# Seven block products for the FFN up projection, down steps between them, modulation sums on the tensor engine

## The chip, the cores and the metric

The kernel runs on one core of one Trainium2 chip. The metric is device time in microseconds (us) of one execution, from several runs. TensorE (PE) multiplies matrices into PSUM; VectorE (DVE), ScalarE (ACT) and GpSimd (POOL) work on elements; the DMA queue of SyncE (SP) brings data from DRAM.

## What is computed

Two layers of a diffusion backbone in float32: 512 tokens x and 256 context tokens, width 1024. A layer is a half-step FFN, a mixer (convolution, gated linear attention, attention), and another half-step FFN. The context's last FFN is not needed, so of four FFNs three have 768 tokens and the last has 512. Cut to what the change touches:

```python
def pre(x, mod, j, g):
    return rms_norm(x, g) * (1 + mod[:, :, 3 * j + 1]) + mod[:, :, 3 * j]

def half_ffn(x, mod, j, g, w1, w2):
    gu = pre(x, mod, j, g) @ w1          # w1: 1024 x (2 x 2816)
    a, u = jnp.split(gu, 2, axis=-1)
    return x + 0.5 * mod[:, :, 3 * j + 2] * ((jax.nn.silu(a) * u) @ w2)

mod_x = (silu(c) @ w_ada[i] + b_ada[i]).reshape(B, 1, 9, 1024)   # and mod_c of c_ctx
```

## The kernel before, in words

Tokens lie along the columns, features along the 128 partitions; 1024 features are eight K tiles. Every float32 matrix product is made of three passes over exact pairs (hi, lo) of reduced float32 (fp32r): hi x hi, hi x lo, lo x hi (`mm3`, L386). A weight tile of 128 x 1024 is loaded by `load_split` (L132): a DMA, a cast on ACT (hi), a subtraction on DVE (lo); three such pairs are in flight.

An FFN (`ffn`, L402) runs over 22 hidden tiles of 128. For each, `up` makes two tiles, a and u: 8 K tiles x 3 passes x 2 column pieces of 386 and 384 columns (768 tokens and two columns that carry the shift). `evac` (L462) multiplies by 1 / rms on DVE and applies silu or the shift on ACT; a product on DVE gives the hidden tile, which is split into a pair (gh, gl). After every two hidden tiles, `down` adds those of the pair before to all eight output tiles (528 matmuls of 512 columns and 528 of 256 per FFN, 528 of 512 in the last) and `add_gated` (L395) adds them to the residual xt on DVE. `Scale` (L336) prepares x * gs as pairs tile by tile as x becomes final.

The modulation vectors (`ada`, L183) are products of a vector by a matrix: ACT scales each K tile of 128 x 512 by its element of silu(c), DVE adds it up, and at the end TensorE sums over partitions (L206). Vectors 2 to 8 of layer 0 are made during the first FFN, 0 to 4 of layer 1 during the second, 5 to 8 during the third. `ada_first` (L211) makes vectors 1 and 0 on TensorE at the start; the first up products begin before the shifts (vector 0) are there (`Head`, `up_head`).

The order on each engine is set by the framework's scheduler, by the order of writing; only stretches under `manual_schedule` keep their written order on TensorE.

```python
    def mm3(outs, w, m, segs, first, last):
        for o, (t0, n) in zip(outs, segs):
            nc.tensor.matmul(out=o, lhsT=w[0], rhs=m[0][:, t0:t0 + n], start=first, stop=False)
        for o, (t0, n) in zip(outs, segs):
            nc.tensor.matmul(out=o, lhsT=w[0], rhs=m[1][:, t0:t0 + n], start=False, stop=False)
```

## Time and profile before

| | us |
|---|---|
| median of 3 runs | 2859.18 |
| lowest and highest run | 2856.81, 2865.5 |
| span of the profiled execution | 2857.3 |
| TensorE busy, of the span | 2781.7 |
| VectorE busy | 1768.5 |
| ScalarE busy | 1200.8 |
| GpSimd busy | 136.4 |

The page gives no time of the profiled execution beside its span, first to last instruction; the median of the runs is 1.9 us above the span. "Busy" of an engine is the union of its instructions; the mean of one matmul includes its overlap with the next, so the rate of matmuls is read from their starts. PEclk is the granted clock of TensorE (1.00 is 2.4 GHz, 0.5 is 1.2 GHz).

### The profile page before, as it was taken

To read this page: it belongs to the slowest core of one execution; us is meant where nothing else is said; L and a number is where in the kernel's file an instruction comes from. 1 tells how busy PE (TensorE), PEld (TensorE's weight loads), DVE (VectorE), ACT (ScalarE), POOL (GpSimd) and SP (SyncE) were. 2 spreads that over 40 slices of the span, in tenths; PEclk is the share of its full clock that TensorE was granted. 3 is DMA by queue.
4 is the path that set the end of the run, shared out by engine and by line. 5 is a ranking of instruction groups with operands and counts; after the bars stand their busy time and mean duration, and the time that the engine had idled before them with its cause. 6 is when DMAs were issued, how large, how long until landed. Compare 5 with 4: busy or idle time off the path is not lost. (4 is left out here: it accounts for less than half of the span.)

```text
span 2857.3 us, 42932 instructions
## 1 busy us (share of the span) xinstructions
PE 2781.7 (97%) x17498; PEld 2541.2 (89%) x17498; DVE 1768.5 (62%) x2974; ACT 1200.8 (42%) x1908; POOL 136.4 (5%) x134
## 2 busy tenths in 40 slices
PE   8999999999899999999999999999999989999999
PEld 4999999988687899999999999999997768999998
DVE  4786874464897565566465746454546588555555
ACT  4665662233347454254252523232324447432322
POOL 1000000010300100000000100000001110100000
PEclk9999999999999999999999999999999999999999
DMA  7443441221211243233231313231312131222322
GB/s 255 144 144 129 141 130 60 67 93 58 65 43 27 86 139 101 82 118 107 78 118 56 116 66 111 74 119 60 98 57 84 47 88 28 91 89 95 98 97 89
DMA packets 98501, 267.67 MB, mean 94 GB/s; under 512 B 11520, under 2 KB 11904, under 8 KB 98304
## 3 DMA queue, kind: packets, MB, share of 16 engines
q1 hardware_dynamic: 98304, 264.93, 28.7%
q8 instruction: 137, 2.24, 0.3%
q14 instruction: 60, 0.49, 0.1%
HBM read 249.16 MB, written 7.34 MB: 90 GB/s over the span
## 5 line engine op out<-in xcount | busy, mean ns | idle before, releaser
L137 ACT CAST whi<-raw 128x1024 fp32r<-128x1024 f32 (+1 forms) x314 | 324.6, 1044 | 1110.8 <-PE up L391 524.2
L389 PE MATMUL up<-sh,whi 128*128 128x386 f32 (+1 forms) x2808 | 691.4, 327 | 2.2 <-ACT sh L362 1.2
L391 PE MATMUL up<-sl,whi 128*128 128x386 f32 (+1 forms) x2808 | 687.8, 325 | 4.7 <-DVE sl L363 4.7
L393 PE MATMUL up<-sh,wlo 128*128 128x386 f32 (+1 forms) x2808 | 686.0, 325 | 0.1
L465 DVE TENSOR_TENSOR upv<-up,rb 128x770 f32<-128x770 f32 (+2 forms) x177 | 157.2, 889 | 639.0 <-PE up L393 634.7
L389 PEld LDWEIGHTS up<-sh,whi 128*128 128x128 f32 x2808 | 493.1, 190 | 12.4 <-ACT whi L137 4.2
L391 PEld LDWEIGHTS up<-sl,whi 128*128 128x128 f32 x2808 | 495.9, 190 | 7.5 <-DVE sl L363 7.3
L393 PEld LDWEIGHTS up<-sh,wlo 128*128 128x128 f32 x2808 | 494.1, 190 | 2.1 <-DVE upv L465 1.7
L399 DVE SCALAR_TENSOR_TENSOR xt<-dn,mods,xt 128x512 f32<-128x512 f32 (+1 forms) x616 | 375.2, 632 | 123.0 <-PE dn L393 122.3
L389 PE MATMUL dn<-gh,whi 128*128 128x512 f32 (+1 forms) x1232 | 429.9, 349 | 3.3 <-DVE xt L399 3.2
L138 DVE TENSOR_TENSOR wlo<-raw,whi 128x1024 fp32r<-128x1024 f32 (+1 forms) x314 | 378.6, 1215 | 83.3 <-ACT whi L137 75.1
L391 PE MATMUL dn<-gl,whi 128*128 128x512 f32 (+1 forms) x1232 | 427.7, 347 | 0.0
L393 PE MATMUL dn<-gh,wlo 128*128 128x512 f32 (+1 forms) x1232 | 426.4, 347 | 0.0
L195 ACT ACTIVATE adat<-adaw,sc 128x512 f32<-128x512 f32 x392 | 258.9, 715 | 84.0 <-DVE adacc L197 76.7
L389 PEld LDWEIGHTS dn<-gh,whi 128*128 128x128 f32 x1232 | 232.8, 189 | 45.0 <-ACT whi L137 7.9
L393 PEld LDWEIGHTS dn<-gh,wlo 128*128 128x128 f32 x1232 | 232.9, 189 | 31.2
L391 PEld LDWEIGHTS dn<-gl,whi 128*128 128x128 f32 x1232 | 233.0, 189 | 29.5
L197 DVE TENSOR_TENSOR adacc<-adacc,adat 128x512 f32<-128x512 f32 x392 | 250.4, 684 | 7.9 <-ACT adat L195 6.3
L468 ACT ACTIVATE upv<-upv 128x512 f32<-128x512 f32 (+1 forms) x308 | 179.7, 625 | 33.8 <-DVE upv L465 33.6
L389 PE MATMUL pj<-nh,whi 128*128 128x512 f32 (+1 forms) x328 | 120.5, 371 | 8.5 <-DVE var L572 4.3
L263 POOL TENSOR_TENSOR acc<-acc,sq 128x512 f32<-128x512 f32 (+1 forms) x72 | 76.1, 1057 | 1075.1 <-ACT sq L260 1069.7
L391 PE MATMUL pj<-nl,whi 128*128 128x512 f32 (+1 forms) x328 | 120.9, 369 | 2.4 <-DVE nl L332 2.3
(216 smaller groups left out, 2798.7 us busy)
## 6 DMA issues: line engine op xcount, KB each, us to landing
raw<-in_w_dram SPq DMA_DIRECT2D x264, 512.0 KB, 3.5
adaw<-in_wada_dram SPq DMA_DIRECT2D x288, 256.0 KB, 3.3
raw<-in_wt_dram SPq DMA_DIRECT2D x26, 512.0 KB, 3.4
raw<-in_wo_dram SPq DMA_DIRECT2D x16, 512.0 KB, 3.6
raw<-in_wk_dram SPq DMA_DIRECT2D x8, 416.0 KB, 3.2
xt<-in_xT_dram SPq DMA_DIRECT2D x8, 384.0 KB, 7.9
park<-xt SPq DMA_DIRECT2D x8, 384.0 KB, 2.3
xt<-park SPq DMA_DIRECT2D x8, 384.0 KB, 5.2
```

The lines of the kernel that those rows point to most:

```text
L137: nc.scalar.copy(out=hi[:, :n], in_=r[:, :n])
L138: nc.vector.tensor_tensor(out=lo[:, :n], in0=r[:, :n], in1=hi[:, :n].bitcast(F32), op=ALU.subtract)
L195: nc.scalar.activation(out=t, in_=r, func=AF.Copy, scale=sc[:, k, v:v + 1])
L197: nc.vector.tensor_tensor(out=acc[v], in0=acc[v], in1=t, op=ALU.add)
L263: eng.tensor_tensor(out=self.acc[:, t0:t0 + n], in0=self.acc[:, t0:t0 + n], in1=s[:, :n], op=ALU.add)
L389: nc.tensor.matmul(out=o, lhsT=w[0], rhs=m[0][:, t0:t0 + n], start=first, stop=False)
L391: nc.tensor.matmul(out=o, lhsT=w[0], rhs=m[1][:, t0:t0 + n], start=False, stop=False)
L393: nc.tensor.matmul(out=o, lhsT=w[1], rhs=m[0][:, t0:t0 + n], start=False, stop=last)
L399: nc.vector.scalar_tensor_tensor(out=x, in0=o[:, :n], scalar=mods[l][:, v, mod * KT + d:mod * KT + d + 1], in1=x, op0=ALU.mult, op1=ALU.add)
L465: nc.vector.tensor_tensor(out=a[:, t0:t0 + n], in0=p[:, c0:c0 + n], in1=rb[:, t0:t0 + n], op=ALU.mult)
L468: nc.scalar.activation(out=a[:, c], in_=a[:, c], func=AF.Silu if t == f else AF.Identity, bias=a[:, NX + v:NX + v + 1])
```

## The change

The up projection is seen as a product of 2 x 2 blocks: weights in rows a and u and in lower and upper half of K (four K tiles each), activations in the two halves of K and two halves of the tokens. Seven block products and sums before and after replace the eight products (`Combos` makes the sums T1 to T4 of activations, `Feed.ups` those of weights on POOL, `Up.product` the sums of results). Each product is 4 K tiles x 3 passes of half the tokens: 386 columns (258 in the last FFN). The sums of results are made in place: a later product accumulates on a PSUM bank that ACT or DVE has written. The order is a list, `PLAN`, in which single down steps (one output tile) stand between products; all engines keep the written order in an FFN. The first two products of the first four hidden tiles come first. 1 / rms is now multiplied on halves, and two columns of shifts ride with each half; the first products need the shifts. Weights lie in rings of their own: units of 128 x 512, five for up and three for down, four raw tiles.

The modulation sums are made on TensorE: four K tiles at a time, each into its own strip of 32 partitions, then a small matmul adds the strips. Constants that only the mixer needs are loaded there. In the mixer, weight splits are in halves of 512; the output projection runs in two token halves.

The core of the diff, first the modulation:

```diff
-                for v in range(nv):
-                    t = acc[v] if k == 0 else slot("F", "adat", (P, 512))
-                    nc.scalar.activation(out=t, in_=r, func=AF.Copy, scale=sc[:, k, v:v + 1])
-                    if k:
-                        nc.vector.tensor_tensor(out=acc[v], in0=acc[v], in1=t, op=ALU.add)
...
+            for k, r in enumerate(nxt):
+                nc.tensor.matmul(out=ps[32 * k:32 * k + 32, :], lhsT=spad[:, 2 * (4 * b + k):][:, :32], rhs=r, start=b == 0,
+                                 stop=b == 1, skip_group_check=True, tile_position=(0, 32 * k))
...
+                for s in range(4):
+                    nc.tensor.matmul(out=ps[:, 2 * s:2 * s + 2], lhsT=a[:, s * P:(s + 1) * P], rhs=sev,
+                                     start=True, stop=True, skip_group_check=True)
```

The sums of activations (`combine`), of weights (`sums`, `one`) and of results (`Up.product`):

```diff
+            def sums():
+                t.append(slot("E", "t13", (P, 2, self.w)))
+                nc.vector.tensor_tensor(out=t[0][:, 0], in0=a[:, 0], in1=b[:, 0], op=ALU.subtract)
+                nc.gpsimd.tensor_tensor(out=b[:, 0], in0=a[:, 1], in1=t[0][:, 0], op=ALU.subtract)
+                nc.vector.tensor_tensor(out=t[0][:, 1], in0=a[:, 1], in1=a[:, 0], op=ALU.subtract)
+                nc.gpsimd.tensor_tensor(out=b[:, 1], in0=b[:, 1], in1=b[:, 0], op=ALU.subtract)
+                self.pair(1, "xt", t[0], tags["13"], ("T1", "T3"), p)
...
+                s1[f] = slot("q", "s1", (P, 512))
+                pool(s1[f], ru[:, lo], ru[:, hi], ALU.add)
+                pool(ru[:, lo], ra[:, lo], ru[:, lo])
...
+                if r == 0:
+                    u = unit(ra[:, lo])
+                    pool(ra[:, lo], s1[f], ra[:, lo])
+                elif r == 1:
+                    u = unit(ra[:, hi])
+                    pool(ra[:, hi], ra[:, hi], ra[:, lo])
...
+                o, name = ((a, "11"), (b, "21"), (d, "T1"), (a, "T2"), (a, "T3"), (c, "22"), (a, "T4"))[r]
+                prod(o, x[name], r in (0, 2))
+                if r == 0:
+                    nc.scalar.copy(out=b, in_=a)
+                elif r == 1:
+                    mul(v0, b, rf[0])
+                elif r == 2:
+                    nc.scalar.copy(out=z[:, 1], in_=d)
+                    if b is not None and self.own:
+                        silu(v0[:, :nh], v0[:, nh:nh + 1])
+                elif r == 3:
+                    add(c, a, z[:, 1])
+                elif r == 4:
+                    add(z[:, 1], a, z[:, 1])
+                    mul(z[:, 1], z[:, 1], rf[1])
+                elif r == 5:
+                    mul(y[:, 1], c, rf[1])
+                else:
+                    for t, n, v in n1:
+                        silu(y[:, 1, t:t + n], (y[:, 1] if v else v0)[:, nh:nh + 1])
+                    mul(z[:, 0], a, rf[0])
+                    gate(z[:, 0, :nh], z[:, 0, nh:nh + 1], v0[:, :nh])
+                    for t, n, v in n1:
+                        gate(z[:, 1, t:t + n], z[:, v, nh:nh + 1], y[:, 1, t:t + n])
```

The product itself, the order, and the weight units:

```diff
+        def prod(o, b, start, post=None):
+            (hi, lo), = feed.get(1)
+            for p in range(4):
+                ws = slice(p * P, (p + 1) * P)
+                for e, (w, m) in enumerate(((hi, b[p][0]), (hi, b[p][1]), (lo, b[p][0]))):
+                    nc.tensor.matmul(out=o, lhsT=w[:, ws], rhs=m, start=start and p == 0 and e == 0,
+                                     stop=p == 3 and e == 2, skip_group_check=True)
...
+        seq = [("h1", f) for f in range(HEADS)] + [("h2", f) for f in range(HEADS)]
...
+            for f in fs:
+                for r in prods:
+                    add(f, r)
+                    if r in (3, 5, 0 if 2 * c >= HEADS else 6) or r == 2 and f > 2:
+                        seq.append(downs.popleft())
+                late.append(("g", f))
...
+        w = wp.tile([P, 2, 512], F32R, tag=tag, name=tag, bufs=RING if tag == "w" else DRING)
+        split(w[:, 0, :n], w[:, 1, :n], src)
```

How the instructions stand now, at three places. **TensorE, inside an FFN.** `up` is a PSUM bank, sh and sl (x22) are activations, whi and wlo (w) a weight pair. Before, the end of one tile and the beginning of the next:

```order
L389 MATMUL up_5231<-sh7_164,whi_5227 128x386
L389 MATMUL up_5231<-sh7_164,whi_5227 128x384
L391 MATMUL up_5231<-sl7_172,whi_5227 128x386
L391 MATMUL up_5231<-sl7_172,whi_5227 128x384
L393 MATMUL up_5231<-sh7_164,wlo_5228 128x386
L393 MATMUL up_5231<-sh7_164,wlo_5228 128x384
L389 MATMUL up_5295<-sh0_157,whi_5291 128x386
L389 MATMUL up_5295<-sh0_157,whi_5291 128x384
```

In the change, the end of the fifth product of a hidden tile, the sixth, the small modulation matmuls and the beginning of a down step:

```order
L649 MATMUL up_521<-xth_610,w_1129 128x386
L649 MATMUL up_521<-xtl_611,w_1129 128x386
L649 MATMUL up_521<-xth_610,w_1129 128x386
L649 MATMUL up_697<-x22_472,w_1164 128x386 x3
L649 MATMUL up_697<-x22_488,w_1164 128x386 x3
L649 MATMUL up_697<-x22_543,w_1164 128x386 x3
L649 MATMUL up_697<-x22_577,w_1164 128x386 x3
L214 MATMUL adapt_1323<-glb_75,adasb_1212 128x2 x4
L461 MATMUL dn_1330<-gh_1043,wd_516 128x512
L463 MATMUL dn_1330<-gl_1044,wd_516 128x512
```

One piece of 386 columns stands where two pieces of 386 and 384 stood, four K tiles make a product, and a down step or modulation work stands between products.

**VectorE, inside an FFN**, before (first FFN; adacc and adat are modulation, wlo a weight's low part, upv an up tile, gl a hidden tile's low part):

```order
L138 TENSOR_TENSOR wlo_783<-raw_780,whi_782 128x1024
L465 TENSOR_TENSOR upv_709<-up_660,rb_173 128x770
L138 TENSOR_TENSOR wlo_842<-raw_839,whi_841 128x1024
L197 TENSOR_TENSOR adacc_903<-adacc_903,adat_911 128x512
L197 TENSOR_TENSOR adacc_904<-adacc_904,adat_914 128x512
L423 TENSOR_TENSOR upv_643<-upv_709,upv_643 128x770
L197 TENSOR_TENSOR adacc_903<-adacc_903,adat_919 128x512
L197 TENSOR_TENSOR adacc_904<-adacc_904,adat_922 128x512
L197 TENSOR_TENSOR adacc_903<-adacc_903,adat_927 128x512
L143 TENSOR_TENSOR gl_715<-upv_643,gh_714 128x770
```

In the change (upz and upy are results of products, rinv is 1 / rms, up and dn are PSUM banks):

```order
L153 TENSOR_TENSOR w_1559<-raw_1264,w_1559 128x512
L655 TENSOR_TENSOR upz_1384<-up_697,upz_1384 128x386
L656 TENSOR_TENSOR upz_1384<-upz_1384,rinv_192 128x386
L153 TENSOR_TENSOR w_1577<-s1_1456,w_1577 128x512
L656 TENSOR_TENSOR upy_1383<-up_521,rinv_192 128x386
L472 SCALAR_TENSOR_TENSOR xt2_198<-dn_1581,mods0_78,xt2_198 128x512
L472 SCALAR_TENSOR_TENSOR xt2_198<-dn_1589,mods0_78,xt2_198 128x256
L153 TENSOR_TENSOR w_1609<-raw_1264,w_1609 128x512
L656 TENSOR_TENSOR upz_1384<-up_697,rinv_192 128x386
L658 SCALAR_TENSOR_TENSOR upz_1384<-upz_1384,upy_1383 128x384
L658 SCALAR_TENSOR_TENSOR upz_1384<-upz_1384,upy_1383 128x128
L658 SCALAR_TENSOR_TENSOR upz_1384<-upz_1384,upy_1383 128x256
```

The modulation sums are gone; between the low parts of weights stand sums of results, and the residual adds of one down step stand between those of two products.

**GpSimd**, before, from the end of the sums for the second FFN's norm to those for the third's (attm belongs to the second layer's mixer):

```order
L263 TENSOR_TENSOR acc_9041<-acc_9041,sq_9477 128x256
L263 TENSOR_TENSOR acc_9041<-acc_9041,sq_9520 128x512
L263 TENSOR_TENSOR acc_9041<-acc_9041,sq_9613 128x256
L741 MEMSET attm0_20212 128x256
L741 MEMSET attm1_20213 128x256
L263 TENSOR_TENSOR acc_14494<-acc_14494,sq_14542 128x512
L263 TENSOR_TENSOR acc_14494<-acc_14494,sq_14555 128x512
```

In the change, inside the first FFN, one hidden tile and the first sum of the next:

```order
L559 TENSOR_TENSOR s1_1456<-raw_1266 128x512
L559 TENSOR_TENSOR raw_1266<-raw_1264,raw_1266 128x512
L559 TENSOR_TENSOR raw_1264<-s1_1456,raw_1264 128x512
L559 TENSOR_TENSOR raw_1264<-raw_1264 128x512
L559 TENSOR_TENSOR s1_1685<-raw_1510 128x512
```

Before, GpSimd had nothing to do while an FFN ran; now it makes four sums of 512 columns for each hidden tile.

## Rows read from the trace of the kernel before

**Rows 1.** The page: busy us of each engine, share of the span, instructions.

```profile
PE 2781.7 (97%) x17498; PEld 2541.2 (89%) x17498; DVE 1768.5 (62%) x2974; ACT 1200.8 (42%) x1908; POOL 136.4 (5%) x134
```

**Rows 2.** Table by stage: FFN, mixer, FFN, FFN, mixer, FFN; busy us, PEclk, DMA.

```profile
core 0: us, PE busy (x) PEld busy (x) DVE busy (x) ACT busy (x) POOL busy (x), PEclk, DMA share, GB/s
60.00:630.00 570.00, 567.03 (x3226) 531.29 (x3226) 385.36 (x578) 288.68 (x435) 11.40 (x13) 1.00 0.36 115
630.00:1018.00 388.00, 363.58 (x2781) 309.34 (x2780) 275.48 (x625) 185.83 (x364) 48.61 (x44) 0.98 0.20 59
1018.00:1588.00 570.00, 568.00 (x3218) 536.86 (x3216) 352.49 (x508) 247.57 (x367) 8.46 (x8) 1.00 0.31 100
1588.00:2165.00 577.00, 573.02 (x3237) 543.60 (x3237) 311.70 (x447) 192.00 (x274) 16.71 (x17) 0.99 0.27 89
2165.00:2475.00 310.00, 284.77 (x2188) 239.88 (x2188) 216.25 (x488) 155.66 (x296) 36.20 (x35) 0.94 0.22 62
2475.00:2853.00 378.00, 377.65 (x2676) 354.82 (x2675) 203.41 (x264) 111.02 (x137) 0.99 (x1) 1.00 0.28 92
```

**Rows 3.** Timeline of TensorE, first FFN: start us, us, engine, line, what.

```profile
300.07 0.39 PE L389 MATMUL dn<-gh,whi 128*128 128x512 f32 x1
300.30 0.40 PE L391 MATMUL dn<-gl,whi 128*128 128x512 f32 x1
...
302.02 0.51 PE L389 MATMUL up<-sh,whi 128*128 128x386 f32 x2
302.37 0.52 PE L391 MATMUL up<-sl,whi 128*128 128x386 f32 x2
```

**Rows 4.** Timeline of TensorE, last FFN.

```profile
2604.57 0.40 PE L389 MATMUL up<-sh,whi 128*128 128x256 f32 x2
2604.80 0.40 PE L391 MATMUL up<-sl,whi 128*128 128x256 f32 x2
```

**Rows 5.** Timeline of TensorE, second FFN, four modulation matmuls (eight records).

```profile
1118.13 0.52 PE L393 MATMUL up<-sh,wlo 128*128 128x386 f32 x2
1118.57 1.07 PE L206 MATMUL adaps<-adacc,one 128*32 128x512 f32 x8
1119.57 0.63 PE L389 MATMUL up<-sh,whi 128*128 128x386 f32 x2
```

**Rows 6.** Timeline of TensorE, first FFN, one modulation matmul (two records).

```profile
86.44 1.05 PE L206 MATMUL adaps<-adacc,one 128*32 128x512 f32 x2
87.42 0.62 PE L393 MATMUL up<-sh,wlo 128*128 128x386 f32 x2
```

**Rows 7.** Groups by line and shape, TensorE: fp32 matmuls with two columns.

```profile
L567 PE MATMUL qst<-glb,qh 128*128 128x2 f32 x80 | 9.8, 247 | 0.2 <-DVE oT L796 0.2
```

**Rows 8.** Groups by line and shape, VectorE: busy us, mean ns, idle before.

```profile
L138 DVE TENSOR_TENSOR wlo<-raw,whi 128x1024 fp32r<-128x1024 f32 x306 | 370.4, 1220 | 56.0 <-ACT whi L137 50.7
L399 DVE SCALAR_TENSOR_TENSOR xt<-dn,mods,xt 128x512 f32<-128x512 f32 x352 | 261.4, 747 | 120.6 <-PE dn L393 119.9
L197 DVE TENSOR_TENSOR adacc<-adacc,adat 128x512 f32<-128x512 f32 x392 | 250.4, 684 | 7.9 <-ACT adat L195 6.3
L465 DVE TENSOR_TENSOR upv<-up,rb 128x770 f32<-128x770 f32 x131 | 125.7, 960 | 514.6 <-PE up L393 510.2 <-PE up L455 4.4
L399 DVE SCALAR_TENSOR_TENSOR xt<-dn,mods,xt 128x256 f32<-128x256 f32 x264 | 125.5, 480 | 2.4 <-PE dn L393 2.4
```

**Rows 9.** Timeline of VectorE and GpSimd, second mixer.

```profile
2298.30 0.74 DVE L905 SCALAR_TENSOR_TENSOR cacc<-hx,cst,cacc 128x512 f32<-128x512 f32 x1
...
2300.26 1.27 POOL L811 TENSOR_TENSOR kh<-kh,glb 128x512 f32<-128x512 f32 x1 [13.79 <-PE qst L567]
2300.56 1.52 DVE L905 SCALAR_TENSOR_TENSOR cacc<-hx,cst,cacc 128x512 f32<-128x512 f32 x1
```

**Rows 10.** Table of one stretch at the start, columns as in rows 2.

```profile
8.00:36.00 28.00, 22.02 (x75) 10.77 (x73) 15.34 (x21) 15.88 (x30) 8.25 (x6) 0.94 1.04 395
```

More of the change, by code (lines that the diff above doesn't have):

```diff
@@ L85 @@
 LA = 2
+HEADS = 4
+RAW = 4
+RING = 5
+DRAW = 2
+DRING = 3
 @with_exitstack
@@ new lines, in later, with step, factors @@
+        def later(self, n, act):
+            self.todo.append((self.steps + n, act))
+        def step(self):
+            self.steps += 1
+            due = [t for t in self.todo if t[0] < self.steps]
+            self.todo = [t for t in self.todo if t[0] >= self.steps]
+            for _, act in sorted(due, key=lambda t: t[0]):
+                act()
+        def factors(self, h, st=None):
+            yield from self.spread(self.half(h), st)
+            nc.scalar.copy(out=self.r[:, h, :self.nh], in_=self.rb[:, :self.nh])
+            yield
@@ new lines, in pair, with high, low @@
+        def pair(self, lag, name, src, tags, names, p):
+            shape = (P, len(names), self.w)
+            made = []
+            def high():
+                made.extend(slot(t, name + "hl"[i], shape, F32R) for i, t in enumerate(tags))
+                nc.scalar.copy(out=made[0], in_=src)
+                for e, n in enumerate(names):
+                    self.x[n][p] = made[0][:, e], made[1][:, e]
+            def low():
+                nc.vector.tensor_tensor(out=made[1], in0=src, in1=made[0].bitcast(F32), op=ALU.subtract)
+            self.later(lag, high)
+            self.later(lag + 1, low)
@@ L1137, in backbone_kernel @@
-    head = Head()
-    for k in range(KT):
-        for seg in [SEGX, SEGC]:
-            nm.feed(seg, k)
-    for seg in [SEGX, SEGC]:
+    advance(first)
+    cb = Combos(0, 0, T // 2, "E")
+    for k in range(KT):
+        xt[k] = slot("A", f"xt{k}")
+        nc.sync.dma_start(out=xt[k], in_=xT_d[:, k, :])
+    advance(first, 2)
+    both = [SEGX, SEGC]
+    halves = [(0, T // 2), (T // 2, T // 2)]
+    for l in range(DEPTH):
+        ends_of[l, 0] = [SEGC, SEGX]
+        ends_of[l, 1] = [SEGX] if l == DEPTH - 1 else halves
```

830 lines of the change are left out of this document (473 added, 357 removed).

## The prediction

> **What bounds the kernel now.** I read the busy times of the engines first, then a table by stage, then the start-to-start times of matmuls, then the prices of the other engines. TensorE is busy 97% of the span, VectorE (DVE) 62%, ScalarE (ACT) 42%, GpSimd (POOL) 5% [rows 1]. By stage [rows 2], TensorE is idle 3 of 570 us in the first FFN, 2 of 570 in the second, 4 of 577 in the third, 0.4 of 378 in the last. The mixers (388 and 310 us) have 24 and 25 us of idle TensorE. So an FFN lasts as long as its matmul stream, and only a shorter stream shortens it. A busy sum is no measure of that stream, since neighbours overlap; starts are. Two matmuls of 386 columns start every 0.35 us, one of 512 every 0.23 [rows 3], two of 256 or 258 in 0.23 [rows 4]. I take 0.176, 0.23 and 0.12 us (0.12 also for the 256-column down matmuls).
>
> Test on the second FFN of before: up has 44 tiles x 8 K tiles x 3 passes x 2 column pieces = 2112 matmuls x 0.176 = 371.7; down 528 x 0.23 + 528 x 0.12 = 184.8; five modulation groups at 1.09 = 5.4. That makes 562 against 570 measured, 1.4% short. I add 1.4% to every full FFN. The last FFN: 2112 x 0.12 + 528 x 0.23 = 374.9 against 378, so 0.9% there.
>
> **The change, part by part.**
>
> *Seven products.* For each of 22 hidden tiles, 7 products x 4 K tiles x 3 passes = 84 matmuls replace 96: 1848 per FFN for 2112, same width and same number of weight loads per matmul. That is 325.2 us for 371.7 in three FFNs and 221.8 for 253.4 in the last: minus 171 us in all. Down stays. Eleven marking matmuls per FFN add 1.9 us (1.3 in the last).
>
> *Modulation on TensorE.* 32 half vectors move there: 14 in the first FFN, 10 in the second, 8 in the third. Each is two groups of four fp32 matmuls into four column strips, then four small ones. A group of four costs 1.09 us: the pair before it starts at 1118.13 and lasts 0.35, the next matmul starts at 1119.57 [rows 5]. One alone costs 0.98 [rows 6], so the four run side by side. The small ones: 80 records of this shape took 9.8 us [rows 7], two records each, four make 1.0. A half vector is 3.2 us: 44, 32 and 25 us. The moved ACT and DVE passes (DVE 250.4 us [rows 8]) win nothing by themselves, for TensorE hid them.
>
> *FFN streams after:* 325.2 + 1.9 + 184.8 + 44 = 556; 544; 537; last 221.8 + 1.3 + 121.4 = 344.5. With the additions 564, 552, 545 and 348.
>
> *DVE and POOL.* Per pair of hidden tiles DVE now has 18 low parts of 512 columns at 0.684, 12 evacuations of 386 at about 0.55 (estimate, between 0.48 for 256 and 0.75 for 512 [rows 8]), about 2.9 of gates, 1.9 for the low parts of the hidden tiles (two of the 770-column size) and 8 x 1.23 of residual adds: 33.5 us, in a TensorE time of 14 x 2.11 + 8 x 2.1 = 46.4 plus modulation. In the last FFN it is 26.6 in 31.1. POOL, unused there before, gets 8 sums of 512 columns, 1.27 each [rows 9], 10.2 us per pair. The trace shows what they collide with: a DVE instruction with two SBUF operands that takes 0.74 alone took 1.52 beside a POOL sum [rows 9]: it waits. In the last FFN such DVE work is 15.6 of the 26.6 us (the rest has a PSUM operand); with POOL 25.8 of 31.1. So it fits, with little room. The Trainium skill, page "SBUF — State Buffer", section "Who interferes with whom", says the same of the mechanism: a DVE instruction with two SBUF inputs and a GpSimd instruction that reads SBUF exclude each other for a whole instruction. The rows agree; the rule speaks against this change, and its strong form is a rival below.
>
> *Waits added.* The sums of the products are formed in place: the fourth accumulates on a bank that ACT has copied, the fifth on one that DVE has just read, and so on. After the first and the fourth product stands a down step (2.1 us; 1.4 in the last FFN), and DVE or ACT needs about 0.6 to 0.8 for its piece. Behind a POOL sum it is 1.27 later, still within 2.1, but 0.3 to 0.5 over in the last FFN. If DVE is late there, TensorE's whole queue stands, down steps included. I take 0 for three FFNs and 22 x 0.4 = 8 us in the last; bounds 0 and two waits of 0.78 per tile. SP's queue issues modulation loads four at a time between weight loads; each waits for the group before on TensorE, four or five steps (9 us) earlier, against a flow of some 6 MB in 50 us (3 MB of weights and three groups of 1 MB per pair), 126 GB/s where 395 were reached [rows 10]: nothing.
>
> *Beginnings of FFNs.* The third product needs differences of both token halves. Before the second, third and fourth FFN, DVE and POOL have, from the last steps of the stage ahead until then, some 34 us of TensorE work to prepare them under; at the third FFN I count for DVE 16 low parts of weights (10.9) and, for each of four K pairs, three sums or parts of 386 and two of 772 columns (0.55 and 0.96; 14.3), some 26 us with two SBUF operands; for POOL 7 squares and 8 differences (0.96 each, 1.27 scaled to 386 columns) and two sums of weights, 17. That is 43, an overrun of 9 if all excludes. I take 5, 5 and 4 us, and bound it by 0 and 15 each. The third also keeps 7 us of its present excess (577 against 562 x 1.014). ACT, busy 248 of 570 us in the second FFN [rows 2], gives up modulation and gets three quarters more weight casts: covered.
>
> *Start.* Scales, x and now also shifts must land before the first product: 11.5 MB (32 x 256 KB, 8 x 384 KB) at 395 GB/s [rows 10] from about 5 us: 34. TensorE follows with its last small matmuls to 39; then splits. The same 26 us of DVE work and the four low parts of the first half (0.96 each), with some 7 of POOL that it waits for, put the third product at about 76 us, with 21 us of stream behind it. Bounds 65 and 88. End of the first FFN: 76 + (556 - 21) x 1.014 = 618, for 630.
>
> *Mixers.* Their matmuls are the same; weights are split in two pieces each: 2 x 0.684 for 1.22 on DVE [rows 8], 0.15 x 25 = 4 us per layer on a DVE that is 71% busy there. I take 3 each; bounds -5 and +12.
>
> **The sum.** First FFN -12; second 552 + 5 = 557 for 570: -13; third 545 + 5 + 7 = 557 for 577: -20; last 348 + 4 + 8 = 360 for 378: -18; mixers +6. Together -57: a span of 2800 for 2857.3. The median of the runs shown is 2859.2, 1.9 more than the profiled span. **Forecast 2802 us.**
>
> **The rivals.**
> 1. *Everything hides.* Start at 65, no new waits: -22, -18, -25, -30 and mixers 0: **2764**. For it: the order puts a down step behind each wait; against: the overrun at the beginnings.
> 2. *POOL and DVE add up fully*, as the page's rule would have it if no DVE work with a PSUM operand fell beside a POOL sum: 26.6 + 10.2 = 36.8 per pair in the last FFN, 11 x 36.8 = 405 for 378, +27 for -18, other FFNs as forecast (43.7 fits 46.4): **2847**. For it: 1.52 against 0.74. Against: 11 of 26.6 us have a PSUM operand.
> 3. *Slower: accumulation waits.* TensorE waits for ACT or DVE in every hidden tile where a product adds to a bank just read. Price: two waits of 0.78 (1.52 - 0.74) per tile, 88 tiles, 137 us, less the 8 counted: **2931**. From 57 / 88 = 0.65 us of wait per tile above the forecast it is slower than before. For it: all engines now follow one written order, so a late ACT copy holds DVE, and DVE TensorE. Against: 2.1 us of cover, and DVE loaded to 72%.
> 4. *The strips do not run side by side*, since their weights now differ by strip: 64 x (4 x 0.98 - 1.09) = 181 more: **2983**. Against it: side by side in [rows 5], with one weight for all strips there.
>
> **How the numbers follow.** Chances: forecast 0.54 (2775 to 2830), rival 1 0.14, rival 2 0.15, rival 3 0.14, rival 4 0.03. Leaving out rivals 3 and 4 leaves out 0.17, and 0.03 may fall outside the rest: the low end is rival 1 with the mixers at -5 each and without the 7 us of the third FFN, the high end rival 2 with 6 us more at the start. The range is **2748 to 2853**. A measurement of this kernel tells about 0.3% from no change. Faster by more than that (under 2850.6): 0.54 + 0.14 and 0.10 of rival 2, with 0.03 of rival 3 at small waits, 0.81; within 0.3%: 0.06; slower: 0.13.
>
> **What would show it.** Right: 1848 up matmuls per FFN at 0.176 (0.12), groups of eight modulation records in 1.09; FFN windows of about 557 (second, third) and 360; TensorE idle at the third product of each FFN; POOL busy about 450 us more, and DVE low parts of twice their length beside it. Wrong: idle before the fifth product in every tile (rival 3), DVE busy throughout the last FFN (rival 2), an FFN window above 570, or a first FFN that ends after 640.

## The result: slower, and the profile after

The changed kernel takes 2940.01 us (median of 4 runs, 2939.25 to 2943.8) where the kernel before takes 2860.46 (4 runs beside it): ratio 1.0283, 95% interval 1.0268 to 1.0299. The forecast was 2802, the range ended at 2853. The profiled execution spans 2942.0 us, 84.7 more than that of before.

The page of the changed kernel, answering to [rows 1] (busy time, then busy tenths and granted clock in 40 slices):

```profile
PE 2765.5 (94%) x17238; PEld 2491.3 (85%) x17238; DVE 1971.3 (67%) x3642; ACT 1180.4 (40%) x2297; POOL 647.5 (22%) x522
...
PE   7699999999989998999999889999998989979998
...
PEclk9899999998999999999999999999998989999999
```

TensorE is busy 16 us less than before and idle 101 us more (176.5 of 2942.0 for 75.6 of 2857.3): that is the whole difference. The busy time would have fallen further at the old clock: over stretches of 10 us, busy time multiplied by what the granted clock lacks of 1 sums to 64 us, before to 30. That sum leaves out the first 78 us, in which TensorE ran at about half its later pace (see The start).

The table by stage, for the stages of [rows 2] (columns as there; I put a boundary where the last down product or output product of a stage ends):

```profile
75.00:692.00 617.00, 579.72 (x3282) 517.25 (x3283) 394.51 (x682) 211.92 (x396) 139.34 (x115) 0.97 0.34 112
692.00:1094.00 402.00, 374.69 (x2766) 323.20 (x2766) 278.00 (x641) 197.22 (x412) 50.65 (x45) 0.94 0.19 58
1094.00:1664.00 570.00, 554.54 (x3182) 511.46 (x3180) 381.42 (x661) 211.21 (x405) 137.32 (x105) 0.99 0.30 101
1664.00:2240.00 576.00, 552.38 (x3135) 508.55 (x3135) 382.43 (x643) 205.90 (x382) 138.68 (x110) 0.98 0.29 96
2240.00:2562.00 322.00, 292.84 (x2219) 246.58 (x2218) 218.61 (x501) 167.77 (x340) 41.90 (x41) 0.93 0.22 65
2562.00:2938.00 376.00, 352.93 (x2392) 326.25 (x2391) 310.23 (x499) 165.62 (x316) 127.32 (x90) 0.98 0.29 95
```

By the same ends of products, the first FFN counted from the start of the span, the stages of before last 630, 386, 576, 573, 315 and 374 us (its second FFN's last down product ends at 1591.9, its last output product at 2479.5, 4 us behind the boundaries of [rows 2]). So the first FFN, which ends at 691.7, is 61 us longer, the mixers are 16 and 7 us longer, and the other three FFNs change by -6, +3 and +2. TensorE, which was idle 3, 2, 4 and 0.4 us in the FFNs, is idle 37, 15, 24 and 23.

Inside an FFN the forecast held. From one pair of hidden tiles to the next (by the residual adds of the down steps) the four FFNs take 51.0, 50.5, 49.7 and 31.25 us, before 52.4, 51.7, 51.5 and 33.95. So over 11 pairs 13 to 30 us are gained per FFN, and lost again at its beginning. The list of waits of TensorE names the places (what it waited for: us in total, times, longest):

```profile
PE up L782 <- DVE head L656: 31.2, 4, 11.9
PE adaps L202 <- DMA adaw<-in_wada_dram: 23.5, 2, 20.5
PE pj L461 <- ACT nh L336: 11.1, 15, 1.6
PE st L290 <- POOL acc L272: 10.2, 3, 8.9
...
PE up L649 <- ACT up L685: 9.8, 6, 6.2
```

**The start.** The timeline of TensorE in the changed kernel:

```profile
27.81 5.26 PE L237 MATMUL adaps<-spad,adaw 128*128 128x2 f32 x24
42.01 1.44 PE L290 MATMUL st<-glb,acc 128*128 128x1 f32 x6 [8.94 <-POOL acc L272]
...
50.38 22.19 PE L237 MATMUL adaps<-spad,adaw 128*128 128x2 f32 x104
74.86 0.69 PE L649 MATMUL up<-xbh,w 128*128 128x386 f32 x1 [2.30 <-ACT w L152]
...
109.78 2.45 PE L202 MATMUL adaps<-adaw,spad 128*32 128x512 f32 x4 [20.50 <-DMA adaw<-in_wada_dram]
...
1105.75 0.73 PE L290 MATMUL up<-glb,acc 128*128 128x1 f32 x6
```

And in the kernel before the matmuls of the scales, and the first up product:

```profile
6.16 12.67 PE L229 MATMUL adaps<-adaw,spad 128*32 128x512 f32 x32 [6.16 <-DMA adaw<-in_wada_dram]
...
21.17 0.84 PE L389 MATMUL up<-sh,whi 128*128 128x386 f32 x2 [1.21 <-ACT sh L362]
```

The scales (m = 1) and shifts (m = 0) are 256 records of 0.21 us, 54.9 us in all. This part of the change is not named ahead of the prediction: the kernel before makes each K tile of these vectors with two matmuls of 512 columns (L229), the changed kernel with eight of two columns (L237). Between them the statistics of x stand in TensorE's order and wait 8.9 us for GpSimd, until 42.0; the last of the shifts' loads had landed at 36.3. The first product comes at 74.9; before it came at 21.2, with the shifts still under way.

About half of these 54.9 us is TensorE's pace. Six records of the statistics (L290) take 1.44 us at 42.0 and 0.73 at 1105.8, where the granted clock is 1.00. Eight records of two columns take 0.95 us at 136.7, 0.12 each, also at 1.00:

```profile
136.69 0.95 PE L214 MATMUL adapt<-glb,adasb 128*128 128x2 f32 x8
```

So up to the first products TensorE worked at about half pace, that of its lower level of 1.2 GHz. The profile gives a granted clock of 1.00 for 0 to 75 us, but the trace's records of the clock begin only at 78.5. In all nine profiles with the small matmuls at the start they begin between 78 and 82 us, in the nine others (the kernel before, and e2 with the runs built on it) between 9 and 15; in each of these, matmuls of 512 columns come first.

After five products TensorE stands 20.5 us before modulation loads. SP's queue at that time:

```profile
80.95 0.33 SPq L130 DMA_DIRECT2D raw<-in_w_dram  x1
82.96 5.35 SPq L135 DMA_DIRECT2D rawd<-in_w_dram  x3
94.71 10.90 SPq L130 DMA_DIRECT2D raw<-in_w_dram  x3
105.70 44.49 SPq L192 DMA_DIRECT2D adaw<-in_wada_dram  x20
150.28 23.09 SPq L130 DMA_DIRECT2D raw<-in_w_dram  x6
```

In these rows the queue issues in the written order. The modulation loads stand behind weight loads that wait for VectorE to empty a buffer; then weight loads stand behind twenty modulation loads that wait for TensorE.

**The third product of an FFN** needs differences of both token halves, and before it a mark (the matmul that opens a PSUM bank for sums in place, L782) on a bank that VectorE must have read. In the second FFN the last head product ends at 1111.5 and the mark starts at 1120.5, 9.0 us later. VectorE in that time:

```profile
1106.15 2.02 DVE L417 TENSOR_TENSOR xtl<-h,xth 128x772 fp32r<-128x772 f32 x1
1108.10 2.06 DVE L417 TENSOR_TENSOR xtl<-t,xth 128x772 fp32r<-128x772 f32 x1
1110.09 0.55 DVE L656 TENSOR_TENSOR head<-up,rinv 128x386 f32<-128x386 f32 x1
...
1113.67 1.21 DVE L153 TENSOR_TENSOR w<-s,w 128x512 fp32r<-128x512 f32 x1 [1.34 <-ACT w L152]
1114.81 0.15 DVE L293 TENSOR_SCALAR var<-up 128x3 f32<-128x3 f32 x1
1114.99 1.04 DVE L159 TENSOR_SCALAR rsq_y<-var 128x3 int32<-128x3 int32 x1
...
1118.86 0.55 DVE L656 TENSOR_TENSOR head<-up,rinv 128x386 f32<-128x386 f32 x1
...
1119.92 0.55 DVE L656 TENSOR_TENSOR head<-up,rinv 128x386 f32<-128x386 f32 x1
```

The last of the eight head products is the second product of the fourth hidden tile. Three things stand ahead of the last two evacuations (L656): low parts that take 2.0 us beside GpSimd's sums (0.95 alone), a weight split that waits for ScalarE, and the root of the second half's statistics (L293 to 1118.9).

**The norm ahead of the mixers** is written K tile by K tile for all engines: VectorE's product, ScalarE's high part, VectorE's low part.

```profile
710.09 0.75 DVE L337 SCALAR_TENSOR_TENSOR nl<-nrm,mods,nh 128x512 fp32r<-128x512 f32 x1 [0.79 <-ACT nh L336]
...
712.29 0.75 DVE L337 SCALAR_TENSOR_TENSOR nl<-nrm,mods,nh 128x512 fp32r<-128x512 f32 x1 [0.79 <-ACT nh L336]
```

A K tile takes 2.2 us, with 0.79 of waiting. Before, the scheduler put three products and then three low parts, 4.0 us for three:

```profile
643.12 2.06 DVE L328 SCALAR_TENSOR_TENSOR nrm<-xt,gs,st 128x512 f32<-128x512 f32 x3 [2.08 <-PE st L291]
645.11 2.07 DVE L332 SCALAR_TENSOR_TENSOR nl<-nrm,mods,nh 128x512 fp32r<-128x512 f32 x3
```

From the last down product until the first projections are through and the token products (tok) run without a break pass 48.5 and 46.1 us, before 33 and 37.

### The profile page after: what moved, and what is told of

The parts are those of the page before. It is cut to its first block, busy times and chain, and to the rows that moved or that the text cites. A ratio compares the mean times of both kernels' runs of the same rounds, so it can differ in the third digit from the quotient of the medians.

```text
span 2942.0 us, 44641 instructions
## 1 busy us (share of the span) xinstructions
PE 2765.5 (94%) x17238; PEld 2491.3 (85%) x17238; DVE 1971.3 (67%) x3642; ACT 1180.4 (40%) x2297; POOL 647.5 (22%) x522
## 4 chain that ended last, share of the span: by engine, by line
PE 81%; DVE 10%; ACT 4%; issue 2%; POOL 2%; DMA 1%; SPq 0%; POOLq 0%; ACTq 0%; DVEq 0%
PE up L649 35%; PE dn L461 7%; PE dn L463 7%; PE dn L465 7%; PE adaps L202 2%; PE upb L649 2%; PE adaps L237 2%; PE pj L461 2%; DVE w L153 2%; PE pj L463 2%; PE pj L465 2%; PE ao L1296 2%; PE s L1262 1%; PE op L463 1%; PE op L461 1%
## 5 line engine op out<-in xcount | busy, mean ns | idle before, releaser
L649 PE MATMUL up<-xth,w 128*128 128x386 f32 (+1 forms) x2560 | 674.1, 330 | 16.1 <-ACT up L685 9.8
L152 ACT CAST w<-raw 128x512 fp32r<-128x512 f32 (+1 forms) x598 | 367.9, 617 | 587.0 <-PE up L649 346.4
L153 DVE TENSOR_TENSOR w<-raw,w 128x512 fp32r<-128x512 f32 (+1 forms) x598 | 431.0, 722 | 147.6 <-ACT w L152 143.9
L472 DVE SCALAR_TENSOR_TENSOR xt<-dn,mods,xt 128x512 f32<-128x512 f32 (+3 forms) x568 | 344.1, 627 | 249.2 <-PE dn L465 248.9
L649 PEld LDWEIGHTS up<-xth,w 128*128 128x128 f32 x2560 | 463.0, 191 | 49.9 <-issue 13.4
L649 PE MATMUL up<-xtl,w 128*128 128x386 f32 (+1 forms) x1280 | 419.0, 327 | 0.0
L463 PE MATMUL dn<-gl,wd 128*128 128x512 f32 (+2 forms) x1092 | 380.2, 348 | 9.7 <-DVE gl L153 9.7
L461 PE MATMUL dn<-gh,wd 128*128 128x512 f32 (+2 forms) x1092 | 382.7, 350 | 1.0 <-DVE xt L472 1.0
L465 PE MATMUL dn<-gh,wd 128*128 128x512 f32 (+2 forms) x1092 | 378.5, 347 | 0.0
L649 PE MATMUL up<-xbh,w 128*128 128x386 f32 (+1 forms) x1344 | 351.2, 330 | 8.1 <-ACT head L761 5.0
L461 PEld LDWEIGHTS dn<-gh,wd 128*128 128x128 f32 x1092 | 207.2, 190 | 39.8 <-issue 14.3
L465 PEld LDWEIGHTS dn<-gh,wd 128*128 128x128 f32 x1092 | 207.2, 190 | 26.5
```

Of the source, the lines that this page charges most:

```text
L152: nc.scalar.copy(out=hi, in_=src)
L153: nc.vector.tensor_tensor(out=lo, in0=src, in1=hi.bitcast(F32), op=ALU.subtract)
L465: nc.tensor.matmul(out=o, lhsT=w[1], rhs=m[0][:, t0:t0 + n], start=False, stop=last)
L472: nc.vector.scalar_tensor_tensor(out=x, in0=o[:, a - t0:b - t0], scalar=mods[l][:, v, mod * KT + d:mod * KT + d + 1], in1=x, op0=ALU.mult, ...
L649: nc.tensor.matmul(out=o, lhsT=w[:, ws], rhs=m, start=start and p == 0 and e == 0, stop=p == 3 and e == 2, skip_group_check=True)
```

## The experiments

Times are medians. The changed kernel is 2938 us beside the kernel before of most of these runs (2857 x 1.0283). "Third product" is the first matmul with a difference as operand; in the changed kernel it starts at 130.4, 1122.1, 1703.5 and 2587.6. Theory A of the expectations is mine after the traces: orders at the beginnings, one queue behind another. Its rivals are the amount of VectorE work, and the TensorE time of modulation.

**e1: the seven early modulation steps of the first FFN later**, from steps 3 to 16 of the written order to steps 10 to 19.

```diff
-            n, first = ticks[0], 2 * HEADS + 8
+            n, first = ticks[0], 2 * HEADS + (11 if early else 8)
...
-                n = early * n // first
+                n = early * max(0, n - 8) // (first - 8)
```

> Only the seven early steps of the first FFN's modulation are moved: from steps 3 to 16 of the written order to steps 10 to 19, behind the eight head products. Theory A (the loss sits at the beginnings, in waits that the written order makes): the two waits of 20.5 and 3.0 us for modulation loads at 89 and 112 us go; the third product, at 129 in the changed kernel, comes at 112 to 117, when VectorE has done the low parts of the differences (107.0) and the head evacuations; 2940 becomes 2920 to 2928. Rival B (the beginnings are bound by the amount of VectorE and GpSimd work, whatever the order): the third product stays at 127 to 130, 2936 to 2944. Rival C (the loss is the TensorE time of modulation itself): no change, 2936 to 2944.

2933.18 us, ratio 1.0266 (1.0249 to 1.0284). The waits for loads are gone and the third product comes at 118.1, 12 us earlier; the first down product gains 8 (166.0 for 174.4), the total 5. Right about the wait, wrong about its worth: most of it had covered the next one.

**e2: the first two vectors in four strips.** 16 matmuls of 512 columns and 8 small ones for each vector, where 64 small ones (128 records) stood.

```diff
-                    for s in range(4):
-                        c = 2 * (4 * half + s)
-                        nc.tensor.matmul(out=ps[:, c:c + 2], lhsT=r[:, s * P:(s + 1) * P], rhs=sc[:, k, :],
...
+                        nc.tensor.matmul(out=ps[32 * k:32 * k + 32, :], lhsT=spad[:, 2 * (4 * b + k):][:, :32], rhs=r,
```

> Modulation vectors 1 and 0 of the first layer as groups of four side-by-side 512-column matmuls (1.09 us a group, 8 groups) in place of 256 small ones of 0.214 us (54.9 us). Theory A: scales are ready at about 18 to 20 us instead of 33, shifts at 38 to 46 instead of 72.6, the first product starts at 42 to 50 instead of 74.9; since the third product still waits for loads that stand behind weight loads and differences, which all move with it, the total falls by 20 to 30: 2910 to 2920. Rival B: the first product moves, the third stays where it is (129), total 2935 to 2944.

2916.29 us, ratio 1.0208 (1.0192 to 1.0223), as theory A had it: first product at 47.3, third at 103.2, 27 us earlier each. This edit is not one of order alone: the two vectors take TensorE 22.8 us where they took 54.9.

**e3: the root of the second half behind the marks** (second to fourth FFN). **e7: six of eight GpSimd sums later.** **e9: both.**

```diff
-                if f == 1:
+                if f == 1 and early:
                     t1 = bigt("up")
                     cb.factor.append(cb.factors(1, t1[:, :512]))
...
             mark([main[n] for n in (0, 1, 3)])
+            if not early:
+                cb.factor.append(cb.factors(1, t1[:, :512]))
+                advance(cb.factor[1])
```

```diff
                 pool(s1[f], ru[:, lo], ru[:, hi], ALU.add)
-                pool(ru[:, lo], ra[:, lo], ru[:, lo])
+                if f > 1:
+                    rest(f)
...
                     u = unit({2: s1[f], 3: ra[:, lo], 4: ru[:, lo], 5: ra[:, hi], 6: ru[:, hi]}[r])
+                    if r == 2 and f < 2:
+                        rest(f)
```

> In the second, third and fourth FFN the statistics and the inverse root of the second token half are put behind the last head evacuation and the marking matmuls (they stood between the second and the third head evacuation in VectorE's order; 4.1 us at 1114.8 to 1118.9). Theory A: the wait at the third product (9.0, 11.9, 9.6 us) is shorter by 4 to 5 us in each of three FFNs and less of the stretch behind it is at the lower clock: 2920 to 2930. Rival B (amount of VectorE and GpSimd work): the same waits, 2936 to 2944. Worse than 2944 if the root of the second half is then late for the evacuation of the fifth product.

> The changed kernel with six of GpSimd's eight weight sums for the first two hidden tiles put behind the weight piece of the third product, so that two instead of eight fall beside VectorE's last low parts of differences. Theory E (collisions): these low parts take 0.95 again instead of 2.0, third product earlier by 3 to 6 us in each FFN, total 2922 to 2932. Rival D: within 3 us of the changed kernel, or worse, since the sums are then late for the fourth product: 2935 to 2945.

> The changed kernel with the edits of e3 and e7 together. Alone neither gained: in e3 the last low parts of differences still took 2.0 us beside GpSimd's sums, in e7 the thirteen small instructions of the root took 7 us (1688.9 to 1695.8) beside the sums that were moved, and stood ahead of the last two head evacuations. Theory F (the two stand in each other's place: either one holds the third product, so only both together move it): third product 7 to 10 us earlier in the second, third and last FFN, 2940 becomes 2905 to 2920. Rival G (the loss moves on again, to ScalarE's copy or the fourth product): 2930 to 2942.

e3: 2938.84 us, ratio 1.0284 (1.0269 to 1.0299); e7: 2939.23, 1.0282 (1.0267 to 1.0297): neither moves the time. VectorE in e7, third FFN, with one line of GpSimd:

```profile
1683.38 0.95 DVE L417 TENSOR_TENSOR xtl<-t,xth 128x772 fp32r<-128x772 f32 x1
...
1689.03 1.04 DVE L159 TENSOR_SCALAR rsq_y<-var 128x3 int32<-128x3 int32 x1
1690.12 2.49 POOL L559 TENSOR_TENSOR raw<-raw 128x512 f32<-128x512 f32 x2
1690.31 1.11 DVE L165 TENSOR_TENSOR rsq_a<-rsq_y 128x3 f32<-128x3 f32 x1
...
1695.35 0.16 DVE L165 TENSOR_TENSOR rsq_a<-rsq_y 128x3 f32<-128x3 f32 x1
...
1695.82 0.55 DVE L663 TENSOR_TENSOR head<-up,rinv 128x386 f32<-128x386 f32 x1
```

The low part is back at 0.95, but the sums now run beside the root, of whose thirteen small instructions five take 1.04 to 1.18 us for some 0.16. Together (e9): 2931.44 us, ratio 1.0264 (1.0249 to 1.0279), 7 us less, inside rival G's range; F expected more. The waits at the marks, 31.2 us in the changed kernel, are 23.0 in e3, 32.8 in e7 and 21.0 in e9. So e3 shortens them without moving the total, and the total moves only with both edits: the two hide each other in part, and a third thing remains.

**e4: the norm's low part one K tile later.**

```diff
-                nc.vector.scalar_tensor_tensor(out=lo, in0=a[:, :n], scalar=shift, in1=hi.bitcast(F32), op0=ALU.add,
+                lows.append(lambda lo=lo, a=a, shift=shift, hi=hi: nc.vector.scalar_tensor_tensor(
...
+                while len(lows) > (1 if k < KT - 1 else 0):
+                    lows.pop(0)()
```

> In the norm ahead of the mixers the low part of K tile k is written behind the scaled copy of K tile k+1, where it stood right behind ScalarE's part of its own tile. Theory A: a K tile of the 512-token block takes 1.5 us instead of 2.2 (VectorE 0.74 + 0.75, no wait of 0.79 for ScalarE): 8 x 0.7 = 5.6 us per mixer, with 2 to 4 more in the tail of the FFN ahead; first projections of 39 to 42 and 37 to 40 us instead of 48.6 and 46.4; 2918 to 2930. Rival B: no change, 2936 to 2944.

2922.84 us, ratio 1.0225 (1.021 to 1.024), as theory A had it. VectorE in e4:

```profile
703.95 0.75 DVE L338 SCALAR_TENSOR_TENSOR nl<-nrm,mods,nh 128x512 fp32r<-128x512 f32 x1
704.62 0.74 DVE L334 SCALAR_TENSOR_TENSOR nrm<-xt,gs,st 128x512 f32<-128x512 f32 x1
705.28 0.75 DVE L338 SCALAR_TENSOR_TENSOR nl<-nrm,mods,nh 128x512 fp32r<-128x512 f32 x1
```

No wait, 1.33 us a K tile; from the last down product to the unbroken token products 35.0 and 36.7 us (48.5 and 46.1). The mixers last 386 and 313 us, as in the kernel before (386 and 315).

**e5: e2 with the vector m = 2 made ahead too.** **e6: first down pieces behind the marks.** **e8: e4 to e7 together.** **e10: only the third piece later.** The edits of e5, e6 and e10 in this order:

```diff
-        for m in (1, 0):
+        for m in (1, 0, 2):
...
-        early = 7 if (l, i) == (0, 0) else 0
+        early = 0
```

```diff
-            feed.dfill(DRING)
             head = {}
...
+            feed.dfill(DRING)
             g, ups = {}, {}
```

```diff
-            feed.dfill(DRING)
+            feed.dfill(DRING - 1)
...
+            feed.dfill(1)
             for f in range(HEADS):
                 e, o = head[f]
```

> As e2, and the vector that the first FFN's residual adds need (m = 2) is made there too, ahead of or among the head products, its loads behind the first weight loads; no modulation step stands in the first 16 steps of the first FFN. Theory A (in the first FFN, weight loads stand in SP's queue behind modulation loads that wait for TensorE, and TensorE stands before modulation loads that wait in SP's queue): against e2 the waits of 18.1 and 2.6 us before the modulation groups and the one of 6.4 us behind ScalarE's copy go; first product at 47 to 56, third product at 85 to 95 (e2: 103.2), first down product at 115 to 130 (e2: 146.2); total 15 to 30 below e2: 2888 to 2903. Rival B (VectorE's work bounds the start): third product within 3 us of e2's, total within 5 of e2.

> The changed kernel with the first three down weight pieces of each FFN split behind the head products and the marks instead of ahead of the first product. Theory D (VectorE and ScalarE lose time at an FFN's beginning on work that is not due: three low parts of 0.68 us and the wait for their load, 2.4 to 3.3 us in the third FFN): third product earlier by 2 to 6 us in the second, third and last FFN, the wait of 4.3 us before the fifth head product of the third FFN gone; 2940 becomes 2925 to 2932. Rival E (only the collisions with GpSimd's sums count): no change, 2935 to 2944.

> e5, e4, e6 and e7 in one kernel. If the loss of the change sits in these orders at the beginnings, as theory A says, the parts add up, with the lower clock behind the waits mostly gone: 2940 - 21 (e2) - 15 to 30 (e5) - 16 (e4) - 5 to 15 (e6, e7) = 2858 to 2883. If one bound stands behind all (amount of VectorE work at the beginnings), they do not add: 2895 to 2915.

> The changed kernel with two instead of three down weight pieces split ahead of the first product, the third behind the fourth head product (its load waits for the first one's buffer). Theory H (ScalarE stands 2.5 us before that load with four head copies and the casts of the differences behind it, VectorE 3.4 us, TensorE 4.3 us): third product of the third FFN 3 to 4 us earlier, of the others 0 to 4, total 2928 to 2936. Rival: as e6, where all three went behind the marks, the wait only moves: 2940 or above.

e5: 2907.01 us, ratio 1.0176 (1.0161 to 1.0192): 9 below e2, third product at 108.4. Neither theory: the loads of m = 2 took buffers that ScalarE's casts of differences need, so another queue stood. e6: 2959.92 us, ratio 1.0351 (1.0334 to 1.0369), 20 slower: theory D falls. ScalarE's copies at the first products now wait for the down weights' loads (TensorE behind them 31.0 us in seven waits, 9.8 in six before). e8, with e6 in it: 2889.57, ratio 1.0115 (1.0099 to 1.013), between the two expectations. e10: 2940.02, 1.0292 (1.0275 to 1.0309), no gain.

**e11: e2, m = 2 ahead, e3 in all FFNs, e4, e7, e10.** **e12: e11 with m = 2 loaded into the eight buffers that are needed last.** **e13: e12 without the low parts of the operands T1 to T4**; the high parts stand in for them, so these products are not exact.

```diff
+        tags = iter((["a2"] * 4 + ["b2"] * 4 + ["d2"] * 6 + ["d1"] * 2) + (["d1"] * 4 + ["a2"] * 4 + ["b2"] * 4 + ["d2"] * 4)
+                    + (["a1"] * 4 + ["b1"] * 4) * 2)
```

```diff
-            self.later(lag + 1, low)
+            if name != "xt":
+                self.later(lag + 1, low)
```

> All edits that theory A asks for, without e6: modulation vectors 1, 0 and 2 of the first layer in strips, the loads of the third ahead of the fifth weight load, the root of the second half behind the marks in all FFNs, the norm's low parts one K tile later, six sums of GpSimd later, the third down piece later. If the loss of the change is made of these orders: first FFN's third product at 80 to 95, second to fourth 7 to 12 us earlier than in the changed kernel, mixers 20 us shorter: 2835 to 2865, level with or below the kernel before (2857). If a single bound stands behind them: 2880 to 2900.

> e11 with the first layer's three vectors loaded into other buffers: those of m = 2 into the eight that the fourth product's operands need last, so that ScalarE's casts of differences no longer wait for modulation matmuls (6.8, 4.0 and 3.7 us at 53 to 69 in e11). Theory A (the rest of the loss in the first FFN is again an order: ScalarE's queue behind buffers that modulation holds): third product at 75 to 88 (e11: 101.4), total 2846 to 2862, level with the kernel before. Rival B (VectorE's amount of work): third product at 98 to 103, total 2870 to 2878.

> e12 without the eight low parts of the operands T1 to T4 at the beginning of each FFN (8 x 0.95 us of VectorE; the high part stands in for the low one, so these products are not exact). Rival B (at the third product TensorE waits for the amount of VectorE's work): third product 6 to 8 us earlier in every FFN, total 22 to 35 below e12. Theory A (chains and orders, VectorE has room): 0 to 3 us per FFN, total within 10 of e12.

e11: 2874.2 us, ratio 1.0058 (1.0043 to 1.0073), e12: 2869.62, 1.0035 (1.0023 to 1.0048). 70 of the 81 us are back, some 22 of them by e2's shorter start and the rest by orders and buffers, though each time less than theory A expected (third product of e12 at 95.6, not 75 to 88). e13: 2852.4 us, 0.9969 (0.9958 to 0.9981): 17 below e12, less than the amount of work would give (22 to 35) and more than orders would (up to 10). So the amount of VectorE's work has a share. The waits at the marks did not fall (25.1 us for 24.4 in e12): the evacuations stand behind weight splits that wait, by way of ScalarE's cast, for GpSimd's sums, and those for loads, as in the second FFN of e13:

```profile
1041.90 1.29 POOL L571 TENSOR_TENSOR s<-raw 128x512 f32<-128x512 f32 x1 [2.95 <-DMA raw<-in_w_dram]
1043.88 1.11 DVE L153 TENSOR_TENSOR w<-s,w 128x512 fp32r<-128x512 f32 x1 [3.08 <-ACT w L152]
```

**e14: no modulation in the second and third FFN.** Constants stand in for the second layer's nine vectors.

```diff
-            ffn(l, 1, cb, both, (ada(1, range(5)), 5), after, feeds[l, 1], feeds[l + 1, 0])
+            ffn(l, 1, cb, both, none, after, feeds[l, 1], feeds[l + 1, 0])
```

> The changed kernel without the nine modulation vectors of the second layer (constants stand in for them): 18 half vectors less in the second and third FFN, with their 36 MB of loads. If modulation costs what its matmuls take (two groups of 1.07 and 0.95 of small ones, 3.1 us a half vector): 56 us less, 2940 becomes 2880 to 2888, the second FFN 31 and the third 25 us shorter. If its loads also hold up weights in SP's queue: over 65 us less, below 2875. If TensorE had idle time for it anyway: under 45 less, above 2895.

2880.56 us, ratio 1.0072 (1.0056 to 1.0089): 57 us less (2857.67 x (1.0283 - 1.0072) = 60 by the ratios). Its matmuls make 58 us (18 x 3.2), so in these FFNs modulation costs its matmuls and at most 2 us more.

**e15: e12 with the head evacuations ahead of the splits for the third to fifth products.** **e16: and ScalarE's copies into the first banks ahead of them as well.**

```diff
-                prod(o, x["21"], False, lambda: mul(e[:, 1], o, rf[0]))
+                prod(o, x["21"], False, lambda: mul(e[:, 1], o, rf[0]), f > 0)
...
+            begin(0)
+            begin(1)
+            feed.fill(1)
             cb.factor.append(cb.factors(1, t1[:, :512]))
             advance(cb.factor[1])
+            feed.fill(2)
```

(`f > 0` keeps the splits back; `begin`, in e16 alone, marks and copies the banks of a hidden tile; `fill` makes the splits.)

> e12 with the four head evacuations ahead of the weight splits for the third to fifth products on VectorE (in e12 they alternate, and a split waits 1.3 us for ScalarE, which waits for GpSimd's sums, which wait for weight loads). Theory J (what is left at the third product is VectorE's in-order queue: evacuations that are ready stand behind splits that wait for loads; this is why taking 7.6 us of work away in e13 brought 1 to 5 us): the wait at the marks, 24.4 us in four in e12, falls below 8; third product 4 to 7 us earlier in each FFN, total 2846 to 2860, level with or below the kernel before. Rival: the products behind then wait for the same splits, and the total stays at 2865 to 2875.

> e15 with ScalarE's copies of the first two head results into their banks, and the marks for them, ahead of the weight splits for the fourth to sixth product. In e15 the wait at the third product went from VectorE's head evacuation (24.4 to 5.2 us) to ScalarE's copy (4.1 to 26.2 us), which stands behind casts that wait for GpSimd's sums. Theory J (in-order queues of VectorE and ScalarE): third product 4 to 6 us earlier in each FFN, the 26.2 us below 8, total 2838 to 2850, faster than the kernel before (2857 to 2859). Rival: the products after it wait for the same casts, total 2857 to 2864.

e15: 2861.52 us, ratio 1.0009 (1.0001 to 1.0018). The wait moved, as ScalarE and the list of waits of e15 show:

```profile
1053.85 0.62 ACT L152 CAST w<-raw 128x512 fp32r<-128x512 f32 x1
1058.21 0.62 ACT L152 CAST w<-raw 128x512 fp32r<-128x512 f32 x1 [3.74 <-POOL raw L570]
1058.73 0.48 ACT L706 COPY up<-head 128x386 f32<-128x386 f32 x1
```

```profile
PE up L667 <- ACT up L706: 26.2, 5, 6.3
...
PE up L801 <- DVE head L677: 5.2, 4, 2.0
```

e16: 2849.3 us, ratio 0.9976 (0.9964 to 0.9987): faster than the kernel before by 0.24%, and 3% faster than the changed kernel, with the same products and sums; of modulation, the first layer's first three vectors are made in strips ahead of the first products. Its waits:

```profile
PE up L667 <- ACT upz L718: 11.4, 6, 4.4
...
PE up L801 <- DVE head L677: 5.6, 4, 2.0
```

## Why the prediction was wrong

Against the forecast span of 2800 the profiled one is 142 us longer. By stages, change measured against change forecast: first FFN +61 for -12, second -6 for -13, third +3 for -20, last +2 for -18, mixers +23 for +6. That makes 73, 7, 23, 20 and 17.

1. **Products, modulation, start-to-start times: right.** The streams were forecast at 552, 545 and 348 us; the pairs run at 50.5, 49.7 and 31.25 us, 11 pairs 556, 547 and 344. A group of four modulation matmuls and the small ones take 1.06 and 0.95 us (the second at 136.69, above):

```profile
141.92 1.06 PE L202 MATMUL adaps<-adaw,spad 128*32 128x512 f32 x8
```

   e14 takes 18 of the 32 half vectors out and gets 57 to 60 us; 18 x 3.2 makes 58. So of the 171 us that the products save modulation gives about 101 back, as written. A group of four in 1.06 us, with different weights in each strip, also settles rival 4.
2. **"Start": wrong, 73 us.** "TensorE follows with its last small matmuls to 39" gave them no price of their own; they end at 72.6, though the loads landed at 36.3 for the 34 of the forecast. Their records take 0.21 us each, where 80 records of that shape took 9.8 us in the mixer [rows 7], 0.12 each, because TensorE runs at about half its pace there; and the statistics stand between them. The third product came at 130.4 for the 76 of the forecast. e2 moved first and third product by 27 us. The rest is the step that put SP's queue at "nothing": I set the loads against the bandwidth of [rows 10]; what counted was which load stands behind which wait. e1 and e5 each took one such wait out and met the next.
3. **"Beginnings of FFNs": wrong, some 50 us in three FFNs.** I took 5, 5 and 4 us as an overrun of VectorE's work, bounded at 15, and let that work run without a gap. In the written order every engine waits for another at every few instructions, and instructions that are ready stand behind one that is late. e15 and e16 show what this is worth: from e12 to e16 only order changes, and 2869.62 becomes 2849.3 (17 us by the ratios). Moving GpSimd's sums alone brings nothing (e7), since the collision moved to the root. Less work does bring something: e13 takes some 30 us of VectorE's work away (8 x 0.95 per FFN, less in the last) and brings 17. How the 50 us divide between order and work is not shown.
4. **"Waits added", 8 us in the last FFN: wrong the other way.** Inside the last FFN TensorE is idle 0.4 of 256 us (2634 to 2890), with no wait before the fifth product, as its cover by a down step said; rival 3, whose 2931 lies nearest to the result, is not what happened, nor rival 2: VectorE is busy 310 of 376 us there.
5. **"Mixers", 3 us each: wrong, 23 in all for 6.** I priced the weight splits and did not see that the norm's order is written out now, since it runs under the FFN's manual schedule. e4 brought 15 us and the mixers back to their old length.
6. **The clock.** I did not count it. By the sums above the lower level adds up to 34 us of busy time after 78 us (64 for 30), and at the start some 23 (256 x 0.09, an estimate from 0.21 and 0.12 us a record); both lie within the losses named here. At 720 to 730, among the waits for the norm, TensorE is busy 9.6 us at a granted clock of 0.50, the level of 1.2 GHz. In e16 the mean is 0.977 for 0.968, before 0.987.

Two of the signs of being wrong came, an FFN window above 570 (the third, 576) and a first FFN that ends after 640 (691.7). The common fault: each gain was read from a stage in its steady state, and the losses lie in the beginnings, the first 130 us of the kernel and the first 30 to 60 us of each later stage, where the trace of before has a scheduler's order and the change a written one.

What stays open: e16 is still 47 us above the forecast. Its first FFN ends at 642 for 618 in the forecast (630 before), its second and third take 1129 us together for 1114 (1149 before), its last 373 for 360 (374 before). How much more the beginnings would give was not tried.

## What to carry to other kernels

When a change replaces the scheduler's order by a written one, walk through the first product of every stage on all engines, in order, with the longest of the latencies ahead of each instruction; a sum of busy times is not enough there. Two suspects can hide each other, so that neither removed alone moves the time (here 0, 0 and 7 us together): try them together before acquitting them. Loads that wait for a consumer and loads that a consumer waits for do not belong in one queue without a look at which comes first.

## What the runs showed of the hardware

A VectorE instruction of three columns, 0.16 us alone, takes up to 1.18 us beside GpSimd's sums of some 1.26 us (e7: a chain of thirteen takes 7 us); a low part of 772 columns takes 2.06 for 0.95. So a collision cost 0.9 to 1.1 us here whatever the size of VectorE's instruction, and weighs most on chains of small ones. The Trainium skill, page "SBUF — State Buffer", section "Who interferes with whom", says that whichever of the two engines comes second blocks fully until the other's instruction is done. These rows agree: no loss is longer than a sum.

Four fp32 matmuls of 512 columns into four strips of 32 partitions run side by side in 1.06 us also with different weights in each strip. Eight such groups (8.5 us) and four times 0.95 us of small ones do in e2 what 256 records of 0.21 us do in the changed kernel.

With two-column matmuls at the start, TensorE kept about half its pace for 78 us: 0.21 us a record for 0.12, 1.44 us for 0.73 in the statistics. With matmuls of 512 columns first, the records of a granted clock of 1.00 begin at 9 to 15 us. Which difference between these starts matters was not tested.
